# FoX head pairs: where the put-off value and sums transposes stand in the matmul order

## The chip, the cores and the metric

The kernel runs on one core of one Trainium2 chip. The metric is the device time of one execution in microseconds; before the change it is 1346.64 us (median of three runs, 1346.08 to 1347.43). Engines are named as the profile names them: PE multiplies matrices (PEld loads its stationary operand), DVE, ACT and POOL work on vectors, SP issues most DMAs.

## The reference, cut to what matters

One layer of a hybrid decoder trunk on 1024 tokens of width 1024. One projection feeds an HGRN2 head group and a FoX head group (softmax attention with a forget-gate bias, 16 heads of width 64). The change touches only the FoX part: the projection that gives v, and the attention.

```python
def fox_branch(q, k, v, fz, fb):
    q, k, v = heads(q), heads(k), heads(v)
    log_f = jax.nn.log_sigmoid(fz.astype(f32) + fb.astype(f32))
    F = jnp.cumsum(log_f, axis=1).transpose(0, 2, 1)
    for blk in range(S // Q):
        logits = (jnp.einsum('bhtd,bhsd->bhts', qb, kb).astype(f32) * scale
                  + F[:, :, q0:q1, None] - F[:, :, None, :q1])
        probs = jax.nn.softmax(jnp.where(mask, logits, -jnp.inf), axis=-1)
        outs.append(jnp.einsum('bhts,bhsd->bhtd', probs.astype(v.dtype), vb))

u = rmsnorm(h, norm_w[i])
proj = jnp.einsum('bsd,de->bse', u, w_in[i])
hq, hf, hi, hg, fq, fk, fv, fg, fz = jnp.split(proj, SPLIT_POINTS, axis=-1)
y_f = fox_branch(fq, fk, fv, fz, fox_fb[i]) * jax.nn.silu(fg)
y = jnp.concatenate([y_h, y_f], axis=-1)
h = h + jnp.einsum('bse,ed->bsd', y, w_out[i])
```

## The kernel before

The kernel runs in stages: a start (norm, per-layer embedding), the HGRN heads, the FoX heads (about 540 to 1075 us in the profile), and the output projection with the gate and the last norm. Activations are kept transposed, features on partitions and tokens along the free dimension.

**Dense products.** A projection to 128 features is a "dense" job of two products of 512 tokens each (`dense_steps`, `product_steps`, line 355). A product is 24 matmuls of 128x512: eight slices of the contraction (index i), and for each three matmuls (index j) of operands split into a high and a low part (whi, wlo, uhi, ulo). Both halves of the work, the dense jobs of the next pair and the attention of this one, go through PE in one order that the code writes out: `pe` (line 353) keeps PE's instructions in program order. The order on the other engines is set by a scheduler when the program is built; each engine then runs its own list strictly in order.

**The planner.** `Ahead` (line 322) holds the dense jobs as generators. `fill(columns)` (line 343) runs matmuls of the first job until a number of columns is used up; `fill()` without a number runs all that is left. A job's eviction of a product out of PSUM comes when the generator is asked for the step behind the product's last matmul. `weights()` hands out the loaded weights and starts the load of the next (wf by DMA, whi by ACT on line 82, wlo by POOL on line 83). `FOX_FILL` (line 34) gives the columns of a fill: 12288, which is 24 matmuls, while pairs 1 to 4 are worked on, and 9216, which is 18, for pairs 0, 5, 6 and 7.

**Pairs and chunks.** Heads come in eight pairs p of two heads i, each in two chunks c of 512 queries, c = 1 first. The chunks run in a row. `Chunk.mix` (line 878) does for one chunk, twice (part 0 and 1): two groups of logits of the following chunk (line 811, tile lg), half of its own softmax (ACT exponentials on line 847, DVE transposes on line 848), and a fill; then the maxima of the following chunk and its own value products (`values`, line 850, tile po, matmuls on line 859). A copy (avt, line 870, ACT) and an addition (line 871, DVE) bring po to the output tile o. During pair p the jobs of pair p+1 are filled in, in the order k, q, (gate of p), v.

**Put-off steps.** Two kinds of small transposes on PE are not issued where their operands arise but put on the list `ahead.pending`:

- *value transposes* (`fox_v`, line 473): each of the two products of v is copied out to vt (line 480, ACT); the step then transposes vt in four matmuls (line 485), copies the result into the tile v (line 487, ACT), and POOL swaps halves of it into the other rows (`swap`, line 444).
- *sums transposes* (`norms`, line 894): once the exponentials of a head are done, its sums zs go through one matmul (line 900), a copy zk (line 904, ACT), an addition and a reciprocal zt (lines 905 and 908, DVE), a DMA out to zd and a DMA back to rz (lines 910 and 911, SP). rz is what o is multiplied with at the end of a pair (line 918, POOL).

The list is emptied (`flush`, line 334) at three places: behind the first matmul of slice i = 2 of any product (line 360), that is behind its 7th matmul; at the end of a pair, behind `fill()` (line 976); and in the last chunk. The tiles of dense products, of value transposes and of sums transposes come from one PSUM pool of two buffers (pp, tag "proj").

At the end of pairs 0 to 6 the last product of v has its eviction only when `fill()` is called behind the value products. So its value transposes are issued there, by the flush at the pair's end.

Of the kernel before, what the change touches and what calls it, by code (L numbers as in the profile page):

```python
# [64 lines left out]
def trunk(ctx: ExitStack, tc: tile.TileContext, a, out):  # L65
# [85 lines left out]
    with ExitStack() as st:  # L151
# [137 lines left out]
        for c in range(NCH):  # L289
            for k in range(KT):  # L290
# [6 lines left out]
                if c == 0 and k in (2, 4, 6, 7):  # L297
                    i = 8 + (2, 4, 6, 7).index(k)
# [23 lines left out]
    class Ahead:  # L322
# [8 lines left out]
            self.loaded = load and load()  # L331
            return w

        def flush(self):

            while self.pending:
                self.pending.pop(0)()

        def until(self, mark):
            while mark not in self.done:  # L340
# [14 lines left out]
    def product_steps(ps, terms, cost):  # L355
        n = len(terms)
        for i, (whi, wlo, uhi, ulo) in enumerate(terms):
            for j, (x, y) in enumerate(((whi, uhi), (whi, ulo), (wlo, uhi))):
                pe(mm(ps, x, y, start=i == j == 0, stop=i == n - 1 and j == 2))  # L359
                if i == 2 and j == 0:  # L360
                    ahead.flush()
                yield cost

    def dense_steps(mov, evac):
        whi, wlo = ahead.weights()
        for c in range(NCH):
            ps = pp.tile([P, CH], F32, name="ps", tag="proj")
            yield from product_steps(ps, [(whi[:, j], wlo[:, j], *mov[c][j]) for j in range(KT)], CH)
            evac(c, ps)

    def w_in_loads():
        tiles = [T_HQ, T_HG]
        for h in range(HEADS_H - 1):
            tiles += [T_HF + h + 1, T_HQ + h + 1, T_HG + h + 1] + ([-(h + 2)] if h % 2 == 0 and h < HEADS_H - 2 else [])
        tiles += [T_FQ, T_FG, T_FK, T_FV]
        for p in range(PAIRS_F - 1):
            tiles += [T_FK + p + 1, T_FQ + p + 1] + ([T_FG + p] if 0 < p < FIRST_LATE else []) + [T_FV + p + 1]
        tiles += [T_FG + p for p in range(FIRST_LATE, PAIRS_F)]
        for t in tiles:
            yield (lambda t=t: load_w(a["w_in"][t], KT)) if t >= 0 else (lambda t=t: load_pair(T_HI - t))  # L380
        yield lambda: load_w(a["w_out"][0], KT, nc.vector)

    ahead = Ahead(w_in_loads(), first_f)
# [45 lines left out]
    def fox_gate(p):  # L429
        sg = sg_t.setdefault(p, None) or fi.tile([P, S], F32, name="sg")  # L430
        sg_t[p] = sg

        def ev_g(c, ps):
            sl = slice(c * CH, (c + 1) * CH)
            nc.scalar.activation(sg[:, sl], ps, AF.Tanh, scale=0.5)
            nc.vector.scalar_tensor_tensor(out=sg[:, sl], in0=sg[:, sl], scalar=1.0, in1=ps, op0=ALU.add, op1=ALU.mult)

        yield from dense_steps(u, ev_g)
        ahead.done.add(("gate", p))

    def swap(dst, src):

        for r in range(2):
            nc.gpsimd.tensor_scalar(out=dst[r], in0=src[r], scalar1=1.0, scalar2=1.0, op0=ALU.mult, op1=ALU.mult)
# [16 lines left out]
    def fox_k(p):  # L461

        k = k_t[p] = [fp.tile([P, S], F32, name="k", tag="k", bufs=4) for _ in range(2)]

        def ev_k(c, ps):
            sl = slice(c * CH, (c + 1) * CH)
            nc.scalar.copy(k[0][:, sl], ps)
            swap([k[1][half[r], sl] for r in range(2)], [k[0][half[1 - r], sl] for r in range(2)])

        yield from dense_steps(u, ev_k)  # L470
        ahead.done.add(("k", p))

    def fox_v(p):


        v = v_t[p] = fp.tile([P, 2 * FB, P], F32, name="v")

        def ev_v(c, ps):
            vt = fp.tile([P, CH], F32, name="vt", tag="tmp")
            nc.scalar.activation(vt, ps, AF.Copy, scale=0.5)  # L480

            def transposes():
                pt = pp.tile([P, CH], F32, name="ps", tag="proj")
                for b in range(4):
                    pe(nc.tensor.transpose(pt[:, b * P : (b + 1) * P], vt[:, b * P : (b + 1) * P], ident))
                dst = v[:, 8 * c : 8 * c + 8].rearrange("p (b r) d -> p b r d", r=2)
                nc.scalar.copy(dst[:, :, 0], pt.rearrange("p (b d) -> p b d", d=P))
                swap([dst[half[r], :, 1] for r in range(2)], [dst[half[1 - r], :, 0] for r in range(2)])

            ahead.pending.append(transposes)  # L490

        yield from dense_steps(u, ev_v)
        ahead.done.add(("v", p))


    with ExitStack() as st:
# [244 lines left out]
        gates, values = [], [(v, None)]  # L741
# [24 lines left out]
    with fox as st:  # L766
# [4 lines left out]
        class Chunk:  # L771
# [122 lines left out]
            def norms(self, rz):  # L894

                zs = z_t[self.head]

                def transpose():
                    pz = pp.tile([P, CH], F32, name="ps", tag="proj")
                    pe(nc.tensor.transpose(pz[: 2 * FB, :P], zs, ident))  # L900
                    zt = fp.tile([2 * FB, 64], F32, name="zt", bufs=1)
                    zk = fp.tile([2 * FB, 64], F32, name="zk", bufs=1)
                    src = pz[: 2 * FB, :P].rearrange("m (h a q) -> m h a q", h=2, a=2)
                    nc.scalar.copy(zk.rearrange("m (h q) -> m h q", h=2), src[:, :, 0])
                    nc.vector.tensor_tensor(
                        out=zt.rearrange("m (h q) -> m h q", h=2), in0=src[:, :, 1], in1=zk.rearrange("m (h q) -> m h q", h=2), op=ALU.add
                    )
                    nc.vector.reciprocal(out=zt, in_=zt)
                    row = zd[self.head : self.head + 1, :]
                    nc.sync.dma_start(out=row.rearrange("o (b t) -> (o b) t", t=64), in_=zt)  # L910
                    nc.sync.dma_start(out=rz[half[self.i]], in_=row.to_broadcast([64, S]))

                ahead.pending.append(transpose)

        def finish(p, by_gate):
            o = y_t[p]
            if not by_gate:
                nc.gpsimd.tensor_tensor(out=o, in0=o, in1=rz_t.pop(p), op=ALU.mult)
            else:
                nc.gpsimd.tensor_tensor(out=o, in0=o, in1=sg_t[p], op=ALU.mult)  # L920
                (nc.sync if p < PAIRS_F - 1 else nc.gpsimd).dma_start(out=yd[KT + p], in_=o)

        def gate_late(p):
            yield from fox_gate(p)
            if p < PAIRS_F - 1:
                finish(p, True)
# [15 lines left out]
        def y_load(pool, tag, bufs, num=1):  # L942
            t = pool.tile([P, num, S], F32, name=f"yf{len(y_f32)}", tag=tag, bufs=bufs)
            for i in range(num):
                nc.sync.dma_start(out=t[:, i], in_=yd[len(y_f32)])
                y_f32.append(t[:, i])

        for n, ch in enumerate(chunks):
            p, i, c = ch.p, ch.i, ch.c
            following = chunks[n + 1] if n + 1 < len(chunks) else None  # L950
            if i == 0 and c == NCH - 1:
                rz_t[p] = fp.tile([P, S], F32, name="rz", bufs=1)
                if p == PAIRS_F - 1:
                    y_t[p] = o7
                    y_t[FIRST_LATE] = fp.tile([P, S], F32, name="olate", tag="k", bufs=4)
                    nc.sync.dma_start(out=y_t[FIRST_LATE], in_=yd[KT + FIRST_LATE])
                    ahead.jobs += [gate_late(p - 2), gate_late(p - 1), fox_gate(p)]
                    for x in ((fp, "k", 4), (fi, "q", 2), (fp, "v", 2, 2)):
                        y_load(*x)
                else:  # L960
                    if p:
                        y_t[p] = fi.tile([P, S], F32, name="o")
                    ahead.jobs += [fox_k(p + 1), fox_q(p + 1)]
                    if 0 < p < FIRST_LATE:
                        ahead.jobs.append(fox_gate(p))
                    ahead.jobs.append(fox_v(p + 1))
            if c == NCH - 1 and n + 2 < len(chunks):
                chunks[n + 2].biases()
            if following and following.p > p:
                ahead.until(("k", p + 1))  # L970
            if n == len(chunks) - 1:
                y_load(fp, "pt1", 1, 4)
            ch.mix(following)
            if i == 1 and c == 0:
                ahead.fill()
                ahead.flush()
                finish(p, False)
                if p == FIRST_LATE:
                    nc.sync.dma_start(out=yd[KT + p], in_=y_t[p])
                elif p != PAIRS_F - 2:  # L980
                    finish(p, True)
# [173 lines left out]
```

## Time and profile before

| what | value |
|---|---|
| median of the runs | 1346.64 us |
| the profiled execution | 1351.1 us |
| its span, first to last instruction | 1349.2 us |
| mean granted clock of PE | 0.982 |
| PE busy in the FoX stage (540 to 1075 us) | 506.86 of 535 us |
| ACT busy there | 234.47 us |
| DVE busy there | 345.22 us |
| POOL busy there | 176.25 us |

Durations below come from the profiled execution. In the timeline a row has the start in us from the span's start, the length in us, the engine, the line of the kernel, the operation with output and inputs, how many instructions it merges, and in brackets how long the engine sat idle before it and what it waited for. SPq is a DMA issued from SP's queue. fp32 matmuls count twice in the profile (L859 x32 are 16 matmuls of the program).

### The profile page before, as it was taken

How to read it: one execution, taken by the hardware profiler on the slowest of the kernel's cores; microseconds unless marked ns; L12 is line 12 of the kernel's file. 1: busy time of each engine (PE TensorE's matmuls, PEld its weight loads, DVE VectorE, ACT ScalarE, POOL GpSimd, SP SyncE). 2: the span in 40 equal slices, each digit the busy share in tenths (PEclk: the TensorE clock that was granted, in tenths of full speed). 3: DMA queues.
4: the chain of work that ended last, by engine and by line, in shares of the span. 5: the costliest groups of instructions: out<-in, count | busy, mean ns of one | idle time of the engine just before them, and what ended most of it. 6: DMA issues, size and time to landing. Idle time of an engine off the chain costs nothing.

```text
span 1349.2 us, 26805 instructions
## 1 busy us (share of the span) xinstructions
PE 1284.5 (95%) x10996; PEld 1024.2 (76%) x10996; DVE 794.6 (59%) x1988; ACT 475.2 (35%) x1144; POOL 350.4 (26%) x288
## 2 busy tenths in 40 slices
PE   6999999999999999998999999999889999999996
PEld 4887888888888878666767676766667688888895
DVE  6746575656646575575656565667586833333465
ACT  5413132212312133444444444444353512212455
POOL 3613122212212122324242424233322200101232
PEclk9899999999999999998999999999899999999998
DMA  7312111101111112112112111211232453212312
GB/s 283 128 47 64 49 32 64 63 18 61 36 46 51 32 48 70 58 56 71 56 64 64 66 62 56 71 56 56 70 97 87 151 208 110 86 52 70 129 68 74
DMA packets 38970, 102.22 MB, mean 76 GB/s; under 512 B 6720, under 2 KB 8896, under 8 KB 38848
## 3 DMA queue, kind: packets, MB, share of 16 engines
q1 hardware_dynamic: 38704, 99.99, 22.3%
q8 instruction: 86, 1.41, 0.4%
q0 software_dynamic: 144, 0.52, 0.1%
q14 instruction: 36, 0.29, 0.1%
HBM read 83.07 MB, written 17.43 MB: 74 GB/s over the span
## 4 chain that ended last, share of the span: by engine, by line
PE 78%; DVE 10%; ACT 7%; issue 2%; DMA 2%; POOL 1%; SPq 0%; DVEq 0%; ACTq 0%; POOLq 0%
PE ps L359 45%; PE lg L811 5%; PE ps L98 4%; PE ps L100 4%; PE ps L99 4%; PE po L859 4%; ACT x L847 3%; DVE x L825 2%; PE ps L566 1%; PE gps L98 1%; PE gps L99 1%; PE gps L100 1%; DVE x L275 1%; PE po L707 1%; PE po L709 1%
## 5 line engine op out<-in xcount | busy, mean ns | idle before, releaser
L359 PE MATMUL ps<-uhi,whi 128*128 128x512 f32 x896 | 362.8, 405 | 0.0
L359 PE MATMUL ps<-ulo,whi 128*128 128x512 f32 x896 | 355.3, 397 | 0.0
L359 PE MATMUL ps<-uhi,wlo 128*128 128x512 f32 x896 | 354.2, 395 | 0.0
L83 POOL TENSOR_TENSOR wlo<-wf,whi 128x1024 fp32r<-128x1024 f32 x59 | 144.6, 2451 | 481.8 <-ACT whi L82 459.6
L359 PEld LDWEIGHTS ps<-uhi,whi 128*128 128x128 f32 x896 | 169.7, 189 | 60.3 <-issue 25.9
L359 PEld LDWEIGHTS ps<-uhi,wlo 128*128 128x128 f32 x896 | 169.8, 190 | 36.6 <-issue 1.1
L359 PEld LDWEIGHTS ps<-ulo,whi 128*128 128x128 f32 x896 | 170.0, 190 | 33.5 <-issue 0.7
L825 DVE CUSTOM_DVE_ANT_0 x<-lg,fb 128x512 f32<-128x512 f32 (+15 forms) x256 | 101.8, 433 | 111.6 <-PE lg L811 104.9
L82 ACT CAST whi<-wf 128x1024 fp32r<-128x1024 f32 (+1 forms) x77 | 79.6, 1035 | 207.5 <-PE ps L99 89.9
L847 ACT ACTIVATE x<-x,mxo 128x512 f32<-128x512 f32 (+15 forms) x256 | 130.3, 511 | 59.5 <-DVE mxo L835 59.5
L848 DVE STREAM_TRANSPOSE pt<-x 128x512 f32<-128x512 f32 (+15 forms) x256 | 115.4, 459 | 36.3 <-ACT x L847 32.3
L98 PE MATMUL ps<-yhi,whi 128*128 128x512 f32 x256 | 99.8, 390 | 1.8 <-DVE h L1007 1.8
L99 PE MATMUL ps<-ylo,whi 128*128 128x512 f32 x256 | 99.7, 390 | 0.2 <-DVE ylo L83 0.2
L100 PE MATMUL ps<-yhi,wlo 128*128 128x512 f32 x256 | 99.6, 389 | 0.0
L811 PE MATMUL lg<-k,q 64*32 64x480 f32 (+15 forms) x1024 | 77.7, 411 | 2.5 <-DVE mx L825 2.5
L811 PE MATMUL lg<-k,qx 64*32 64x512 f32 (+15 forms) x1024 | 78.2, 413 | 0.0
L859 PEld LDWEIGHTS po<-pt,v 64*64 64x64 f32 x1536 | 53.6, 133 | 22.7 <-issue 9.2
L859 PE MATMUL po<-pt,v 64*64 64x256 f32 (+7 forms) x1536 | 69.4, 320 | 0.0
L98 PEld LDWEIGHTS ps<-yhi,whi 128*128 128x128 f32 x256 | 48.0, 188 | 12.2 <-ACT whi L82 2.2
L99 PEld LDWEIGHTS ps<-ylo,whi 128*128 128x128 f32 x256 | 48.0, 188 | 10.4 <-DVE ylo L83 0.6
L100 PEld LDWEIGHTS ps<-yhi,wlo 128*128 128x128 f32 x256 | 48.1, 188 | 10.0
L359 PE MATMUL ps<-wthi,uhi 128*128 128x256 f32 x192 | 54.0, 281 | 0.0
(205 smaller groups left out, 2160.6 us busy)
## 6 DMA issues: line engine op xcount, KB each, us to landing
wf<-in_w_in_dram SPq DMA_DIRECT2D x64, 512.0 KB, 3.5
fb<-fd SPq DMA_DIRECT2D x64, 128.0 KB, 3.0
yf<-yd SPq DMA_DIRECT2D x16, 512.0 KB, 5.6
wf<-in_w_out_dram SPq DMA_DIRECT2D x16, 512.0 KB, 3.6
x<-in_xT_dram SPq DMA_DIRECT2D x8, 512.0 KB, 9.4
pled<-pleo SPq DMA_DIRECT2D x16, 256.0 KB, 2.9
yd<-sg SPq DMA_DIRECT2D x8, 512.0 KB, 2.6
rz<-zd SPq DMA_DIRECT2D x16, 256.0 KB, 3.4
```

What stands on the lines that cost most here:

```text
L82: pin(nc.scalar.copy(hi, src))
L83: pin(lo_engine.tensor_tensor(out=lo, in0=src, in1=hi, op=ALU.subtract))
L98: pin(mm(ps, whi, uhi, start=i == 0, stop=False))
L99: pin(mm(ps, whi, ulo, start=False, stop=False))
L100: pin(mm(ps, wlo, uhi, start=False, stop=i == n - 1))
L275: nc.vector.scalar_tensor_tensor(out=x, in0=x, scalar=norm_w[:, k : k + 1], in1=rs[c], op0=ALU.mult, op1=ALU.mult)
L359: pe(mm(ps, x, y, start=i == j == 0, stop=i == n - 1 and j == 2))
L811: mm(ps[32 * j : 32 * j + 32, m % 2, : 32 * n], q[:, 32 * (j // 2) :][:, :32], k[not own][rows].rearrange("p (t a k) -> p t a k", a=2, k=3 ...
L825: nc.vector.tensor_tensor_reduce(out=x, in0=ps[:, m % 2, : 32 * n], in1=copies[m % 2][:, : 32 * n], scale=1.0, scalar=BIG, op0=ALU.add, op ...
L847: nc.scalar.activation(x, x, AF.Exp, bias=self.other[:, g : g + 1], scale=-1.0, accum_out=zs[:, m : m + 1])
L848: nc.vector.transpose(self.probs[:, : m + 1, g], x.rearrange("p (t k) -> p t k", k=32))
L859: mm(po[half[t % 2], r, 32 * first : 256], v_t[self.p][half[r], t ^ r, half[self.i]], self.probs[half[r], t, first:].rearrange("p g q -> p ...
```

## The change

The list now holds a kind beside each step ("values" or "sums"), and `flush` can be told which kinds and how many. Inside a product there are three places for a step instead of one, behind the 7th, the 13th and the 19th matmul, and each place issues at most one step, the oldest. At a pair's end only steps of the kind "sums" are issued; a value step that is left stays on the list until the next dense product. The last chunk still empties the whole list.

```diff
@@ class Ahead
-        def flush(self):
-
-            while self.pending:
-                self.pending.pop(0)()
+        def put_off(self, kind, step):
+            self.pending.append((kind, step))
+
+        def flush(self, *kinds, most=None):
+
+            steps = [x for x in self.pending if not kinds or x[0] in kinds][:most]
+            self.pending = [x for x in self.pending if x not in steps]
+            for _, step in steps:
+                step()
@@ product_steps
-                if i == 2 and j == 0:
-                    ahead.flush()
+                if i in (2, 4, 6) and j == 0:
+                    ahead.flush(most=1)
@@ fox_v
-            ahead.pending.append(transposes)
+            ahead.put_off("values", transposes)
@@ Chunk.norms
-                ahead.pending.append(transpose)
+                ahead.put_off("sums", transpose)
@@ the loop over the chunks
             if i == 1 and c == 0:
                 ahead.fill()
-                ahead.flush()
+                ahead.flush("sums")
                 finish(p, False)
```

Lines behind `flush` move down by five (L485 is L490 after the change, L359 is L364). What moves on PE stands the same way at the ends of pairs 0 to 6. At the end of pair 0, PE's order before, around the value products (po), the value transposes (from vt) and the first logits of pair 1's second chunk (lg):

```order
L359 MATMUL ps_5962<-uhi_305,wlo_5647 128x512
L859 MATMUL po_6043<-pt0_5876,v_5289 64x256 x4
...
L859 MATMUL po_6043<-pt0_5876,v_5289 64x32 x2
L485 MATMUL ps_6065<-cst_307,vt_6063 128x128 x4
L811 MATMUL lg_6090<-k_5461,qx_5643 32x256
...
L811 MATMUL lg_6102<-k_5460,q_5642 32x160
L359 MATMUL ps_6130<-uhi_275,whi_5853 128x512
L359 MATMUL ps_6130<-ulo_276,whi_5853 128x512
```

and after the change:

```order
L364 MATMUL ps_5962<-uhi_305,wlo_5647 128x512
L864 MATMUL po_6043<-pt0_5876,v_5289 64x256 x4
...
L864 MATMUL po_6043<-pt0_5876,v_5289 64x32 x2
L816 MATMUL lg_6082<-k_5461,qx_5643 32x256
...
L816 MATMUL lg_6094<-k_5460,q_5642 32x160
L364 MATMUL ps_6122<-uhi_275,whi_5853 128x512
...
L364 MATMUL ps_6122<-uhi_279,whi_5853 128x512
L490 MATMUL ps_6130<-cst_307,vt_6063 128x128 x4
L364 MATMUL ps_6122<-ulo_280,whi_5853 128x512
```

The four value transposes moved from ahead of the logits to behind the 7th matmul of the next dense product.

In the product before that one, the last of pair 0, both kinds of steps are on the list. PE's order there before (value transposes from vt, then the sums transpose from zs), and after:

```order
L359 MATMUL ps_5962<-uhi_295,whi_5646 128x512
L485 MATMUL ps_6002<-cst_307,vt_5960 128x128 x4
L900 MATMUL ps_6010<-cst_307,zs_5419 16x128
L359 MATMUL ps_5962<-ulo_296,whi_5646 128x512
L359 MATMUL ps_5962<-uhi_295,wlo_5647 128x512
```

```order
L364 MATMUL ps_5962<-uhi_295,whi_5646 128x512
L490 MATMUL ps_6002<-cst_307,vt_5960 128x128 x4
L364 MATMUL ps_5962<-ulo_296,whi_5646 128x512
...
L364 MATMUL ps_5962<-uhi_299,whi_5646 128x512
L905 MATMUL ps_6016<-cst_307,zs_5419 16x128
L364 MATMUL ps_5962<-ulo_300,whi_5646 128x512
```

The second step moved six matmuls down. In pairs 1 to 4 the sums come first and the value transposes are the ones that move down; pairs 5 and 6 are like pair 0.

ACT's order at the end of pair 0 before (exponentials of the next chunk on tile x1, the weight cast whi, the copies avt and vt), and after:

```order
L904 COPY zk_6013<-ps_6010 16x64
L847 ACTIVATE x1_5914,zs_5746<-x1_5914,mxo_6036 128x512
...
L847 ACTIVATE x1_5914,zs_5746<-x1_5914,mxo_6036 128x352
L82 CAST whi_6126<-wf_6124 128x1024
L847 ACTIVATE x1_5914,zs_5746<-x1_5914,mxo_6036 128x320
L847 ACTIVATE x1_5914,zs_5746<-x1_5914,mxo_6036 128x288
L870 COPY avt_6060<-po_6043 64x512
L480 ACTIVATE vt_6063<-ps_5962 128x512
```

```order
L852 ACTIVATE x1_5914,zs_5746<-x1_5914,mxo_6036 128x512
L909 COPY zk_6019<-ps_6016 16x64
...
L82 CAST whi_6118<-wf_6116 128x1024
L852 ACTIVATE x1_5914,zs_5746<-x1_5914,mxo_6036 128x384
...
L852 ACTIVATE x1_5914,zs_5746<-x1_5914,mxo_6036 128x320
L875 COPY avt_6060<-po_6043 64x512
L485 ACTIVATE vt_6063<-ps_5962 128x512
L852 ACTIVATE x1_5914,zs_5746<-x1_5914,mxo_6036 128x288
```

vt and avt moved ahead of the last exponential, zk behind the first, the cast two exponentials up. This is so at pairs 0, 5 and 6; at pairs 1 to 4 avt and vt stay behind the last exponential.

On SP, at pairs 0, 5 and 6, the DMA of rz (line 911) moved behind the next weight load (line 88): before, the three DMAs stood in the order zd, rz, wf; now in the order zd, wf, rz. That weight load waits for the buffer that POOL's wlo (line 83) reads. On POOL, one of the two swaps of v at pairs 0, 5 and 6, and both at pairs 1 to 4, now stand behind the multiplication of o with rz, and at pairs 1 to 4 behind the one with the gate too.

## The prediction

> **What bounds the kernel now.** I read the page first, for the share of each engine, then the waits of PE in the FoX stage (540 to 1075 us), then the timeline at single pair ends, and last the granted clock around them.
>
> ```profile
> span 1349.2 us, 26805 instructions
> PE 1284.5 (95%) x10996; PEld 1024.2 (76%) x10996; DVE 794.6 (59%) x1988; ACT 475.2 (35%) x1144; POOL 350.4 (26%) x288
> ```
>
> PE is the bound: it is busy for 95% of the span, so a microsecond counts when it is taken from PE's waits or from the length of its matmuls. The waits of PE in the FoX stage (what waited, on what; microseconds in all, times, longest) are these four groups:
>
> ```profile
> PE ps L485 <- ACT vt L480: 18.8, 7, 3.9
> PE ps L485 <- DVE zt L905: 4.8, 4, 1.2
> PE lg L811 <- DVE mx L825: 2.5, 5, 1.0
> PE ps L900 <- ACT v L487: 2.0, 3, 0.7
> ```
>
> Three of the four stand before a put-off step: the value transposes (L485) and the sums transpose (L900). Together they are 18.8 + 4.8 + 2.0 = 25.6 us in 14 places, and seven of these are the ends of pairs 0 to 6. The timeline shows why, at the end of pair 0 (start, length, what; idle time before it in brackets):
>
> ```profile
> 608.39 0.28 PE L900 MATMUL ps<-cst,zs 128*16 128x128 f32 x1 [0.68 <-ACT v L487]
> 608.71 0.20 ACT L904 COPY zk<-ps 16x64 f32<-16x64 f32 x1 [0.37 <-PE ps L900]
> 612.49 1.31 PE L859 MATMUL po<-pt,v 64*64 64x256 f32 x32
> 614.27 1.03 ACT L82 CAST whi<-wf 128x1024 fp32r<-128x1024 f32 x1
> 615.76 0.52 ACT L847 ACTIVATE x<-x,mxo 128x288 f32<-128x288 f32 x1
> 616.40 0.58 ACT L870 COPY avt<-po 64x512 f32<-64x512 f32 x1
> 617.00 0.60 ACT L480 ACTIVATE vt<-ps 128x512 f32<-128x512 f32 x1
> 617.65 1.11 PE L485 MATMUL ps<-cst,vt 128*128 128x128 f32 x4 [3.85 <-ACT vt L480]
> ```
>
> PE has nothing left after the value products (po) at 613.80, because the next instruction in its order is the value transposes. They need vt, which ACT does last: the exponentials of the next chunk's softmax, a weight cast and avt stand ahead of it, and it ends at 617.60. The logits of the next chunk, ready to run, are queued behind.
>
> The stall has a second price. The windows below each run from the value transposes of a pair end to the logits behind the first stretch of dense matmuls (columns: length, busy time of PE, PEld, DVE, ACT, POOL, granted clock, DMA share, GB/s). The work in one is transposes, two groups of logits and 24 dense matmuls (18 in the last three).
>
> ```profile
> 617.65:627.13 9.48, 9.48 (x68) 6.78 (x75) 1.90 (x11) 0.58 (x1) 6.13 (x6) 0.74 0.32 113
> 687.22:695.96 8.74, 8.74 (x61) 6.17 (x61) 1.90 (x11) 0.59 (x1) 6.69 (x6) 0.80 0.28 105
> 756.05:763.23 7.18, 7.17 (x61) 5.39 (x61) 1.90 (x11) 0.59 (x1) 6.73 (x6) 1.00 0.23 73
> 823.33:832.10 8.77, 8.77 (x61) 6.29 (x61) 1.90 (x11) 0.59 (x1) 6.70 (x6) 0.81 0.31 105
> 892.19:898.02 5.83, 5.83 (x55) 4.26 (x55) 1.90 (x11) 0.59 (x1) 5.60 (x6) 1.00 0.29 93
> 950.69:959.42 8.73, 8.73 (x54) 6.06 (x54) 1.90 (x11) 0.58 (x1) 3.75 (x5) 0.63 0.33 120
> 1012.10:1020.86 8.76, 8.76 (x54) 6.08 (x54) 1.90 (x11) 0.58 (x1) 3.74 (x5) 0.63 0.51 181
> ...
> 540.00:615.00 75.00, 72.62 (x734) 50.44 (x732) 51.56 (x174) 33.52 (x97) 24.00 (x26) 1.00 0.17 54
> 623.00:687.00 64.00, 61.19 (x609) 44.65 (x607) 38.39 (x134) 27.86 (x83) 17.48 (x18) 1.00 0.18 59
> 692.00:823.00 131.00, 125.34 (x1258) 91.58 (x1256) 78.69 (x278) 56.36 (x167) 41.91 (x40) 1.00 0.19 62
> 828.00:949.00 121.00, 114.77 (x1211) 82.75 (x1209) 79.09 (x274) 53.45 (x161) 38.97 (x39) 1.00 0.20 63
> 958.00:1011.00 53.00, 49.19 (x555) 34.68 (x553) 39.55 (x131) 25.40 (x79) 13.90 (x16) 1.00 0.28 81
> 1019.00:1075.00 56.00, 54.75 (x528) 40.97 (x527) 43.72 (x118) 29.35 (x79) 12.85 (x6) 1.00 0.31 104
> ```
>
> After five of the seven ends the granted clock is below 1; everywhere else in the stage it is 1.00. The two ends that kept it give the undisturbed lengths, 7.18 us with 24 matmuls and 5.83 us with 18. The excess is 2.30, 1.56 and 1.59 us for pairs 0, 1 and 3, and 2.90 and 2.93 us for pairs 5 and 6: 11.3 us in all.
>
> **The change part by part.** The instructions of each kind stay the same; some move.
>
> (a) *Value transposes at a pair end.* They leave the place ahead of the next logits and stand behind the 7th matmul of the next dense product. The wait of 18.8 us goes, and what can be late next is vt at the new place. When PE gets there is read at pair 2, whose clock is full:
>
> ```profile
> 748.48 0.66 PE L485 MATMUL ps<-cst,vt 128*128 128x128 f32 x4 [1.18 <-DVE zt L905]
> ...
> 756.05 0.66 PE L485 MATMUL ps<-cst,vt 128*128 128x128 f32 x4 [1.81 <-ACT vt L480]
> 756.64 0.40 PE L811 MATMUL lg<-k,qx 64*32 64x256 f32 x1
> ...
> 757.55 0.51 PE L359 MATMUL ps<-uhi,whi 128*128 128x512 f32 x1
> ...
> 759.28 0.39 PE L359 MATMUL ps<-ulo,whi 128*128 128x512 f32 x1
> ```
>
> The logits take 757.55 - 756.64 = 0.91 us and seven dense matmuls 759.28 - 757.55 = 1.73 us, so PE reaches the transposes 2.64 us after the values' end. Pairs 0, 5 and 6: the values end 0.68 us sooner by (b), at 613.12 for pair 0, and PE arrives at 615.76. ACT now does vt ahead of the last exponential (616.40 - 615.76 = 0.64 us earlier) and with one small copy, zk, more ahead of it (0.20 us): it ends at 617.16, the transposes start 0.05 us later, and PE waits 1.45 us. Pairs 1 to 4: at pair 2 the stall began at 756.05 - 1.81 = 754.24 and begins 1.18 us sooner by (b); PE arrives at 755.70, and vt, whose place hardly moves, releases it at 756.05: 0.35 us, and about the same (0.36) in the four. New waits: 3 x 1.45 + 4 x 0.36 = 5.8 us. Their bounds are 0 and the old 18.8; I take 5.8, since PE's arrival and the end of vt both come from rows. Queued behind a waiting transpose are the other 17 (or 11) matmuls of the product, nothing else.
>
> (b) *Two steps in one product.* Before, both put-off steps stood behind the 7th matmul, and the second waited for the buffer that the first one's copy releases: 4.8 us (pairs 1 to 4) and 2.0 us (0, 5, 6). Now the second stands six matmuls later, 6 x 0.23 = 1.4 us; the waits were at most 1.25 and 0.68 us, so both go: 6.8 us. Below that, six matmuls cover them; if a copy is late the whole 6.8 us could come back, and no more.
>
> (c) *The clock.* With the long stall gone I expect no drop, a gain of 11.3 us. The bounds are 0 and 11.3. In this trace waits of 0.28 to 1.25 us at a time (the mx, zt and v groups) have no drop behind them, two of four waits of 1.8 us have one, three of three of 3.85 us have a longer one. The new waits, 1.45 us and shorter, lie nearer to the group without.
>
> (d) *Other queues.* On SP, at the ends of pairs 0, 5 and 6, the load of the inverse sums (rz) now stands behind a weight load (wf) that waits for POOL; on POOL one or both swaps of v stand behind the multiplications of o that need rz. Whoever waits is PE, for v, at the value products of the next pair's first chunk. At pair 5:
>
> ```profile
> 945.42 0.45 SPq L911 DMA_DIRECT2D rz<-zd  x1
> 948.48 2.35 POOL L83 TENSOR_TENSOR wlo<-wf,whi 128x1024 fp32r<-128x1024 f32 x1 [5.64 <-ACT whi L82]
> 950.86 0.35 SPq L88 DMA_DIRECT2D wf<-in_w_in_dram  x1
> 950.84 2.38 POOL L918 TENSOR_TENSOR o<-o,rz 128x1024 f32<-128x1024 f32 x1
> 953.30 1.29 POOL L444 TENSOR_SCALAR v<-v 64x512 f32<-64x512 f32 x2
> ...
> rz<-zd SPq DMA_DIRECT2D x16, 256.0 KB, 3.4
> ...
> 964.21 2.16 PE L859 MATMUL po<-pt,v 64*64 64x256 f32 x34
> ```
>
> The weight cast moves two exponentials forward, so wlo ends near 949.9 instead of 950.83; wf is issued, and rz near 950.3, landing 3.4 us later at 953.7, or near 955 if it shares the engines with wf. Then o (2.4 us) and the second swap (0.65) end at 956.8 to 958.2. PE needed 964.21 - 950.69 = 13.52 us from the transposes to po; less the clock's 2.90 and the 2.64 us that now lie ahead of them it is 7.98, so it arrives at 950.25 + 7.98 = 958.2. I cost it at nothing, with bounds 0 and 1 us at each of three ends; the cover is thin, and each microsecond beyond costs one. Pairs 1 to 4 keep their order of DMAs, and the swaps wait only for one more multiplication (2.4 us).
>
> Sum: 25.6 - 5.8 + 11.3 = 31.1 us. The profiled execution took 1351.1 us, so it would take 1320.0; the median of the runs, 1346.64, is 4.5 us lower, and the same difference gives **1315.5 us**.
>
> **The rivals.**
>
> *The clock still falls at some ends.* Two drops followed waits of only 1.8 us while two equal waits left the clock alone, so their place in time seems to matter, and 1.45 us with 0.59 us of transposes behind may do it too, at pairs 0, 5 and 6; or the drops of pairs 1 and 3 had another cause and stay. The price is 1.56 to 1.59 us for each short drop: two to five of them give 1315.5 + 3.2 to 8 = 1318.7 to 1323.5, and the full 11.3 us 1326.8. Against it: every drop in the stage follows a stall. The Trainium skill, TensorE: Matmul & The Clock Gate, "Why this matters for your kernels", asks for "No PE-idle gaps >~3µs between matmul bursts"; by that rule only the 3.85 us stalls could have dropped the clock, and the sum would be 1318.7 us. The trace disagrees at two of the four 1.8 us waits (clock 0.80 and 0.81). The same page, "Part 4: PE-mode transpose", says that transposes do not count as busy for the gate, which would lengthen each gap by its transposes; no run here shows that apart.
>
> *The wait only moves.* If vt is put off on ACT as PE moves on, the transposes stand in the middle of the product as long as before, and the change does not do what it says. For it: they still need the same vt. Against it: PE has 2.64 us of work to put ahead. Price: all of (a) but not (b): 1346.64 - 6.8 = 1339.8, or 1328.5 with the clock's gain.
>
> *Late v.* The swaps come 1 to 3 us too late at pairs 0, 5 and 6: 1318.5 to 1324.5.
>
> *Slower than before.* The same chain, rz behind wf, o behind rz, v behind o, outweighs the gain. It decides from 31.1 / 3 = 10.4 us of lateness at each of the three ends, that is if rz lands about 14 us after its issue where the row has 3.4 us: 1347 us and more. Only the order of the queues speaks for it.
>
> **How the numbers follow.** Forecast (1311 to 1318): 0.59. Clock falls at some ends: 0.21. Late v: 0.08. The wait only moves: 0.06. Slower: 0.03. A new wait smaller than costed or a gain elsewhere, below 1311: 0.03. The range from 1309.5 to 1328 takes in the zero wait of (a) (1309.7) and the full loss of the clock's gain (1326.8) and leaves out about 0.1. About 0.2% (2.7 us) is what a measurement of this kernel can tell from no change. Faster by more: 0.95; within: 0.02; slower: 0.03.
>
> **What would show it.** (a): the wait of L485 for vt near 6 us instead of 18.8, none ahead of the logits at pair ends. (b): the groups waiting for zt and for v gone. (c): granted clock 1.00 through the whole FoX stage and some 7.2 or 5.8 us in windows like those above. (d): no wait of po for POOL. The prediction is wrong if po waits at the first chunk of pairs 1, 6 and 7, if the logits meet a new wait for mx, or if a half clock shows behind short waits.

## The result, and the profile after

| | before | after |
|---|---|---|
| median of four runs each | 1347.04 us (1346.08 to 1348.14) | 1318.72 us (1317.97 to 1319.91) |
| ratio of the runs, 95% interval | | 0.9776 (0.9761 to 0.9791) |
| profiled execution, its span | 1351.1, 1349.2 us | 1317.97, 1316.2 us |
| mean granted clock of PE | 0.982 | 0.994 |

The change makes the kernel 28.3 us faster, with an interval of 28 to 32 us; 31.1 us was forecast. The median of before is now that of four runs; the prediction started from the first three, 1346.64 us. The page's engine row, after:

```profile
PE 1270.2 (97%) x10996; PEld 1014.5 (77%) x10996; DVE 799.8 (61%) x1988; ACT 475.0 (36%) x1144; POOL 351.2 (27%) x288
```

As many matmuls as before take 14.3 us less busy time (1284.5 - 1270.2), which points to the clock; where these 14.3 us lie is shown further down. The waits of PE in the FoX stage, after (what waited, on what; us in all, times, longest):

```profile
PE ps L490 <- ACT vt L485: 6.4, 7, 1.5
PE lg L816 <- DVE mx L830: 2.6, 5, 1.0
```

The groups for zt (4.8 us) and for v (2.0 us) are gone, and the one for vt is 6.4 us instead of 18.8. The timeline at the end of pair 0, PE and ACT:

```profile
614.16 0.58 ACT L875 COPY avt<-po 64x512 f32<-64x512 f32 x1
614.76 0.60 ACT L485 ACTIVATE vt<-ps 128x512 f32<-128x512 f32 x1
615.25 0.53 ACT L852 ACTIVATE x<-x,mxo 128x288 f32<-128x288 f32 x1
...
615.41 0.66 PE L490 MATMUL ps<-cst,vt 128*128 128x128 f32 x4 [1.53 <-ACT vt L485]
```

PE still arrives before vt is ready, but waits only 1.53 us, since the logits and seven dense matmuls of the next product now stand ahead of the transposes. The granted clock in windows of the changed kernel that cover the FoX stage (columns as before; the clock is the third number from the end):

```profile
540.00:612.00 72.00, 71.51 (x758) 49.45 (x756) 49.45 (x172) 32.15 (x93) 22.50 (x24) 1.00 0.16 49
612.00:622.00 10.00, 8.47 (x71) 6.50 (x68) 6.17 (x23) 5.00 (x13) 4.86 (x4) 1.00 0.25 80
622.00:677.00 55.00, 55.00 (x561) 39.95 (x567) 37.70 (x126) 24.49 (x76) 18.67 (x19) 1.00 0.22 69
677.00:690.00 13.00, 12.53 (x114) 9.62 (x99) 7.83 (x33) 5.79 (x16) 9.68 (x8) 1.00 0.30 107
690.00:926.00 236.00, 234.29 (x2473) 169.28 (x2472) 155.64 (x541) 106.33 (x315) 81.96 (x79) 1.00 0.20 64
926.00:938.00 12.00, 10.47 (x88) 7.77 (x91) 9.44 (x32) 4.79 (x13) 6.69 (x6) 1.00 0.26 86
938.00:1055.00 117.00, 111.65 (x1106) 81.79 (x1099) 91.26 (x253) 57.68 (x161) 31.91 (x27) 1.00 0.39 131
```

No drop is left, at the ends of pairs 0, 1 and 5 (second, fourth and sixth window) or elsewhere. And the queues at pair 5, on SP, POOL and PE:

```profile
928.73 0.35 SPq L88 DMA_DIRECT2D wf<-in_w_in_dram  x1
929.18 0.45 SPq L916 DMA_DIRECT2D rz<-zd  x1
...
934.20 2.42 POOL L923 TENSOR_TENSOR o<-o,rz 128x1024 f32<-128x1024 f32 x1 [2.94 <-DMA rz<-zd]
936.70 0.61 POOL L449 TENSOR_SCALAR v<-v 64x512 f32<-64x512 f32 x1
...
937.11 3.03 PE L864 MATMUL po<-pt,v 64*64 64x256 f32 x64
```

rz does stand behind the weight load and POOL does wait for it (2.94 us), as forecast. The second swap ends at 937.31, 0.2 us after PE has begun the value products (937.11), and PE waits for nothing there.

### The profile page after: what moved, and what is told of

It is laid out like the page before. It is cut to its first block, busy times and chain, and to the rows that moved or that the text cites. A ratio compares the mean times of both kernels' runs of the same rounds, so it can differ in the third digit from the quotient of the medians.

```text
span 1316.2 us, 26795 instructions
## 1 busy us (share of the span) xinstructions
PE 1270.2 (97%) x10996; PEld 1014.5 (77%) x10996; DVE 799.8 (61%) x1988; ACT 475.0 (36%) x1144; POOL 351.2 (27%) x288
## 4 chain that ended last, share of the span: by engine, by line
PE 80%; DVE 9%; ACT 6%; issue 2%; DMA 1%; POOL 1%; SPq 0%; DVEq 0%; ACTq 0%; POOLq 0%
PE ps L364 46%; PE lg L816 5%; PE ps L100 4%; PE po L864 4%; PE ps L98 4%; PE ps L99 4%; ACT x L852 2%; PE ps L571 1%; PE gps L100 1%; PE gps L99 1%; PE gps L98 1%; DVE x L275 1%; PE po L712 1%; PE po L714 1%; DVE x L830 1%
## 5 line engine op out<-in xcount | busy, mean ns | idle before, releaser
L364 PE MATMUL ps<-uhi,whi 128*128 128x512 f32 x896 | 360.1, 402 | 0.0
L364 PE MATMUL ps<-ulo,whi 128*128 128x512 f32 x896 | 354.4, 396 | 0.0
L364 PE MATMUL ps<-uhi,wlo 128*128 128x512 f32 x896 | 352.5, 393 | 0.0
L364 PEld LDWEIGHTS ps<-uhi,whi 128*128 128x128 f32 x896 | 168.2, 188 | 58.5 <-issue 21.6
L364 PEld LDWEIGHTS ps<-uhi,wlo 128*128 128x128 f32 x896 | 168.4, 188 | 35.6 <-issue 1.1
L364 PEld LDWEIGHTS ps<-ulo,whi 128*128 128x128 f32 x896 | 168.4, 188 | 33.6 <-issue 0.7
L98 PE MATMUL ps<-yhi,whi 128*128 128x512 f32 x256 | 99.8, 390 | 1.7 <-DVE h L1012 1.7
L816 PE MATMUL lg<-k,q 64*32 64x480 f32 (+15 forms) x1024 | 74.4, 396 | 2.6 <-DVE mx L830 2.6
L816 PE MATMUL lg<-k,qx 64*32 64x512 f32 (+15 forms) x1024 | 74.4, 396 | 0.0
L98 PEld LDWEIGHTS ps<-yhi,whi 128*128 128x128 f32 x256 | 48.0, 188 | 12.2 <-ACT whi L82 2.1
L364 PE MATMUL ps<-wthi,uhi 128*128 128x256 f32 x192 | 54.0, 281 | 0.0
```

The lines of the kernel that those rows point to most:

```text
L98: pin(mm(ps, whi, uhi, start=i == 0, stop=False))
L816: mm(ps[32 * j : 32 * j + 32, m % 2, : 32 * n], q[:, 32 * (j // 2) :][:, :32], k[not own][rows].rearrange("p (t a k) -> p t a k", a=2, k=3 ...
```

## The experiments

The theory: PE is the bound; the gain is the waits before put-off steps (25.6 - 6.4 = 19.2 us) plus the clock that the stalls at pair ends cost. Its rivals: the drops of the clock have another cause; the wait only moves; v comes late. The kernel before was timed beside each of them, on the same chip.

**One part of the change alone.** First the flush at a pair's end, with the old place inside a product (these two edits start from the changed kernel):

```diff
-                if i in (2, 4, 6) and j == 0:
-                    ahead.flush(most=1)
+                if i == 2 and j == 0:
+                    ahead.flush()
```

> Only the flush at a pair's end is changed (sums alone); inside a product both put-off steps stay behind the 7th matmul. Theory (the gain is the pair-end wait plus the clock that it costs): the 6.8 us of waits for zt and v stay, the 18.8 us for vt become about 3 x 1.2 us (PE brings 2.64 us of work ahead of transposes whose vt is as late as before), the granted clock is 1.00 through the FoX stage; 15 us of waits and about 9 us of clock, so about 1323 us. Rival (the clock does not depend on the stall): 15 us, about 1332 us. Rival (the wait only moves): about 1347 us.

Measured: 1324.46 us beside 1350.72 us of the kernel before, a ratio of 0.9807 (0.9793 to 0.9820), 26.3 us less where about 24 were expected. The granted clock is 1.00 through the FoX stage. The waits of PE in this kernel:

```profile
PE ps L490 <- DVE zt L910: 4.8, 4, 1.2
PE ps L490 <- ACT vt L485: 3.5, 3, 1.2
PE lg L816 <- DVE mx L830: 2.5, 5, 1.0
PE ps L905 <- ACT v L492: 2.0, 3, 0.7
```

The waits that the second part would take are untouched, vt costs 3.5 us (3.6 expected), and 18.8 - 3.5 = 15.3 us of waits leave 26.3 - 15.3 = 11 us for the clock (9 expected). Both rivals fall: they had a gain of 15 us and none.

Then the places inside a product alone, with everything issued at a pair's end:

```diff
-                ahead.flush("sums")
+                ahead.flush()
```

> Only the places inside a product are changed (one step behind the 7th, the next behind the 13th matmul); a pair's end still issues everything. Theory (at a pair's end PE waits for ACT, which does not care how early PE comes): the waits for zt and v, 6.8 us, go, but the wait for vt grows by as much less what ACT brings forward (0.64 us less zk at pairs 0, 5 and 6): about 24 us of waiting for vt, the clock drops stay, a gain of 0 to 1.5 us, 1345.5 to 1347 us. Rival (the two parts add up): 6.8 us less, 1340 us.

Measured: 1352.46 us beside 1350.72, a ratio of 1.0020 (1.0009 to 1.0031): not a gain but a small loss. The waits of PE and, in the windows behind it, the clock after the ends of pairs 0 to 6:

```profile
PE ps L490 <- ACT vt L485: 25.4, 7, 4.3
PE lg L816 <- DVE mx L830: 2.6, 5, 1.0
```

```profile
616.50:623.50 7.00, 6.69 (x48) 4.70 (x49) 2.69 (x12) 1.36 (x4) 2.90 (x3) 0.58 0.38 116
688.00:694.00 6.00, 6.00 (x43) 4.50 (x28) 1.85 (x10) 0.00 (x0) 4.79 (x4) 0.78 0.26 91
756.00:761.00 5.00, 5.00 (x46) 3.33 (x45) 1.84 (x10) 0.59 (x1) 4.77 (x4) 0.71 0.32 105
824.00:831.00 7.00, 6.76 (x46) 4.71 (x47) 2.14 (x11) 0.77 (x2) 6.35 (x6) 0.53 0.24 75
895.00:900.00 5.00, 5.00 (x44) 3.64 (x44) 1.85 (x10) 0.59 (x1) 4.77 (x4) 0.66 0.35 108
954.00:960.00 6.00, 5.95 (x44) 4.07 (x45) 2.43 (x12) 1.10 (x3) 2.54 (x3) 0.50 0.41 131
1015.00:1021.00 6.00, 5.97 (x49) 4.24 (x50) 2.40 (x12) 1.08 (x3) 2.05 (x3) 0.73 0.86 268
```

The 6.8 us of waits for zt and v went, and the wait for vt grew by 6.6 us, from 18.8 to 25.4: PE came earlier to the same late vt. The two parts do not add up. The loss of 1.7 us, which I had not expected, goes with the clock: in the profiled execution it fell behind all seven ends, where the kernel before kept it at pairs 2 and 4.

**The clock by itself.** Matmuls whose result nobody reads are put into the stall of the kernel before. In the trace the order of ACT and DVE stays as it was; on POOL the multiplication with the gate moves ahead of a swap at some pair ends. So it is PE's idleness that changes. Added ahead of the flush at a pair's end:

```diff
+                if following:
+                    idle = lg.tile([P, 2, CH], F32, name="lg", tag="lg")
+                    for _ in range(6 if 0 < p < 5 else 14):
+                        pe(mm(idle[:, 0], u[0][0][0][:, :P], u[0][1][0], start=True, stop=True))
```

> The kernel before, with matmuls of 128x512 whose result nobody reads put into the stall at each pair's end (14 at pairs 0, 5 and 6, 6 at pairs 1 to 4), ahead of the value transposes. They need no more than the stall (14 x 0.23 = 3.2 us in 3.85 us), so waits and order stay as before and only PE's idleness is changed. Theory (the idle stall drops the granted clock): clock 1.00 through the FoX stage and 7 to 11 us less, about 1338 us. Rival (the drops have another cause): same time within 2 us.

Measured: 1339.87 us beside 1350.72, a ratio of 0.9920 (0.9908 to 0.9932): 10.9 us less for 66 more matmuls (3 x 14 + 4 x 6). The end of pair 0 on PE (filler, then value transposes), and the stage's clock:

```profile
612.70 1.31 PE L859 MATMUL po<-pt,v 64*64 64x256 f32 x32
613.93 3.47 PE L979 MATMUL lg<-uhi 128*128 128x512 f32 x14
617.87 0.66 PE L485 MATMUL ps<-cst,vt 128*128 128x128 f32 x4 [0.47 <-ACT vt L480]
```

```profile
540.00:1076.00 536.00, 521.50 (x5217) 377.46 (x5216) 352.71 (x1173) 236.60 (x683) 177.93 (x167) 1.00 0.23 76
```

From the end of the value products to the value transposes it is 3.86 us (614.01 to 617.87), against 3.85 us before, so the stall is as long, only filled. The idle stall drops the clock, and that costs 10.9 us (9 to 12 by the interval), against 11.3 us read from the windows of one execution.

The same with transposes as filler:

```diff
-                    for _ in range(6 if 0 < p < 5 else 14):
-                        pe(mm(idle[:, 0], u[0][0][0][:, :P], u[0][1][0], start=True, stop=True))
+                    for _ in range(9 if 0 < p < 5 else 23):
+                        pe(nc.tensor.transpose(idle[:, 0, :P], ident, ident))
```

> As the kernel with dense filler, but the filler is transposes of 128x128 (23 and 9 of them, 0.14 to 0.15 us each) instead of dense matmuls. If any work on PE counts against the drop of the clock, as in the dense filler: about 1338 us and clock 1.00. If transposes do not count as busy, as the Trainium skill says (TensorE: Matmul & The Clock Gate, Part 4: PE-mode transpose): the drops stay, about 1347 us. The theory of the clock leaves this open.

Measured: 1340.01 us beside 1350.72, a ratio of 0.9920 (0.9908 to 0.9932), like the dense filler. The end of pair 0 and the clock behind it:

```profile
613.90 2.73 PE L979 MATMUL lg<-cst 128*128 128x128 f32 x23
617.84 0.66 PE L485 MATMUL ps<-cst,vt 128*128 128x128 f32 x4 [1.21 <-ACT vt L480]
```

```profile
617.84:624.00 6.16, 6.16 (x56) 4.82 (x57) 1.90 (x11) 0.59 (x1) 5.93 (x6) 1.00 0.31 106
```

Transposes keep the clock up, with 1.21 us of idleness left here; the granted clock is 1.00 behind the other pair ends too.

**What is left.** PE still waits 6.4 us for vt. The runs that go after it were timed on two other chips, each beside the kernel before. First the changed kernel itself:

> The changed kernel itself, beside the same runs of the kernel before as the two that follow. Theory (waits 25.6 - 6.4 = 19.2 us, and the clock that the dense filler measured, 10.9 us): 30.1 us less than the kernel before, about 1320.6 us where that one takes 1350.7. Rival (the clock's part is the 9.1 us that the first comparison left): 28.3 us less.

Measured: 1319.86 us beside 1351.22, a ratio of 0.9775 (0.9759 to 0.9790): 31.4 us less, nearer to 30.1 than to 28.3. The ratio is nearly that of the first comparison (0.9776), whose interval (28 to 32 us) holds the theory's figure and the rival's, so theory and rival cannot be told apart.

To take the 6.4 us too, the places were moved six matmuls down:

```diff
-                if i in (2, 4, 6) and j == 0:
+                if i in (4, 6) and j == 0:
```

> The changed kernel with its places for put-off steps behind the 13th and the 19th matmul instead of the 7th, 13th and 19th. Six matmuls more (1.36 us) lie ahead of the value transposes of a pair's end, and ACT brings vt another exponential forward at pairs 0, 5 and 6, so the 6.4 us of waits for vt go. Theory (v is only just ready at pairs 5 and 6, because rz stands behind a weight load): PE then waits there for POOL's swaps, which now both stand behind the multiplication with rz and end about 2.3 us after PE arrives; 6.4 - 4.6 = about 2 us less than the changed kernel, and a new wait of po for POOL near 4.6 us. Rival (PE alone counts): 6.4 us less and no wait for POOL.

Measured: 1317.00 us beside 1351.22, a ratio of 0.9754 (0.9738 to 0.9770), 2.9 us less than the changed kernel. The amount fits, but for another reason. The waits of PE, and POOL and PE at pair 5:

```profile
PE ps L490 <- DVE zt L910: 2.6, 4, 0.6
PE ps L905 <- ACT v L492: 2.1, 3, 0.7
PE ps L98 <- DVE h L1012: 1.7, 1, 1.7
PE lg L816 <- DVE mx L830: 1.1, 2, 0.8
```

```profile
936.26 1.32 POOL L449 TENSOR_SCALAR v<-v 64x512 f32<-64x512 f32 x2
...
936.00 3.03 PE L864 MATMUL po<-pt,v 64*64 64x256 f32 x64
```

The wait for vt is gone (L98 is the stage behind). The 4.6 us of waiting for POOL that I expected are not there: po starts at 936.00 while the swaps run until 937.58. The value products of this chunk go through 16 key slots in order, and the half of v that is swapped last belongs to slots 8 to 15, so it is needed about half of 3.03 us later. Instead the second put-off step now waits for zt and v again (2.6 + 2.1 us), since ACT copies zk and v one exponential later in this kernel's order: at pair 0, v stood ahead of the first exponential and now stands behind it. By the groups: 6.4 - 2.6 - 2.1 + (2.6 - 1.1, fewer waits for mx) = 3.2 us.

With the sums first on the list:

```diff
+            steps = sorted((x for x in self.pending if not kinds or x[0] in kinds), key=lambda x: x[0] != "sums")[:most]
```

> The later places, and where both kinds are on the list the sums first. Then rz is asked for ahead of the weight load at pairs 0, 5 and 6 too, and the multiplication of o with it starts some 4 us sooner. Theory: no wait for vt, none for POOL, 6.4 us less than the changed kernel and faster than both. Rival (v is late for another reason than rz): a wait of po for POOL stays, about 2 us less than the changed kernel.

Measured: 1314.58 us (1313.36 to 1314.77) beside 1351.22, a ratio of 0.9734 (0.9718 to 0.9750) and 5.3 us less than the changed kernel timed with it (1319.66 to 1319.97). The waits for v are gone as well; the four for zt stay:

```profile
PE ps L490 <- DVE zt L910: 2.6, 4, 0.6
PE ps L98 <- DVE h L1012: 1.7, 1, 1.7
PE lg L816 <- DVE mx L830: 1.1, 2, 0.8
```

By the groups, 6.4 - 2.6 + (2.6 - 1.1) = 5.3 us, as measured. No run had a wait of po for POOL that an earlier rz could have taken away; what changed is which of the two steps meets which copy. Two more runs, on the other of these two chips, go further. The second place three matmuls further down:

```diff
-                if i in (4, 6) and j == 0:
+                if i in (4, 7) and j == 0:
```

> As the later places with the sums first, but the second place is behind the 22nd matmul instead of the 19th. The profile of that kernel still has four waits of about 0.65 us for zt before the second step (pairs 1 to 4); three matmuls more are 0.68 us. Theory (a put-off step costs PE only what it comes early): those 2.6 us go and nothing else is late, a ratio to the kernel before of 0.9715, some 2.5 us less than with the 19th. Rival (zt moves on as the step does): the same time as with the 19th, a ratio of 0.9734.

Measured: 1310.90 us (1310.15 to 1311.93) beside 1350.02, a ratio of 0.9712 (0.9699 to 0.9725), 39.1 us faster than the kernel before and the lowest ratio of all. It was not timed beside the run with the 19th, and the two intervals overlap; that the 2.6 us went is read from the waits, of which only these are left:

```profile
PE ps L98 <- DVE h L1012: 1.7, 1, 1.7
PE lg L816 <- DVE mx L830: 1.1, 2, 0.8
```

And the sums first with the places of the change:

```diff
-                if i in (4, 6) and j == 0:
+                if i in (2, 4, 6) and j == 0:
```

> The changed kernel with its own three places (7th, 13th, 19th matmul), only that the sums go first where both kinds are on the list. Theory (v was never late, rz did not cost PE anything): the wait for vt at pairs 0, 5 and 6 shrinks by what ACT brings forward, one exponential of about 0.65 us each, and all else stays: 1 to 2 us less than the changed kernel, a ratio of 0.976 to 0.977. Rival (an early rz was what made the later places pay): most of their gain already here, a ratio near 0.974.

Measured: 1318.21 us beside 1350.02, a ratio of 0.9763 (0.9749 to 0.9776). Its waits before put-off steps:

```profile
PE ps L490 <- ACT vt L485: 3.9, 7, 0.7
...
PE ps L490 <- DVE zt L910: 0.5, 3, 0.2
```

2.5 us less of waiting for vt and 0.5 us more for zt. The ratio lies in the range expected, and its interval still holds the changed kernel's 0.9775. By the waits, the order alone takes 2.0 us, the later places alone took 3.2 us, and both together 5.3 us, so most comes from the places; the times alone do not separate the three.

## Why the prediction was right, point by point

The mechanism and each term were right. The time was not quite: 1318.72 us lies 0.7 us above the forecast of 1311 to 1318. By the time alone it would be the first rival with two short drops (1318.7); the granted clock of 1.00 in its profile rules that out.

*(a), value transposes at a pair's end.* Right. 5.8 us of new waits were forecast, 6.4 measured: 1.53 us at pair 0 (1.45 forecast) and 0.43 to 0.47 us at pairs 1 to 4 (0.36). The run with this part alone shows it by itself.

*(b), two steps in one product.* The 6.8 us of waits went, as forecast. But the sum treated them as a gain of their own, and the run with this part alone shows that they are none: 6.6 of them moved into the wait for vt. In the sum this was right because (a) already counted PE's earlier arrival, 0.68 or 1.18 us, against itself.

*(c), the clock.* The mechanism is shown by the two fillers. Its size, 11.3 us, was that of one execution; the filler measured 10.9 us. The clock differs from run to run: on the chip of the fillers the slowest run of the kernel before, 1352.67 us, has a mean clock of 0.982, and the fastest, 1347.40 us, one of 0.987. The Trainium skill (TensorE: Matmul & The Clock Gate, "Why this matters for your kernels") puts the limit at gaps over about 3 us; the traces agree for the long gaps and differ below, since two of four gaps of 1.8 us had a drop behind them.

*(d), other queues.* Right that it costs nothing. PE was forecast to arrive 7.98 us after the transposes and came after 7.91 (937.11 - 929.20). rz landed later than its median of 3.4 us: POOL waited for it until 5.0 us after its issue. By the prediction's own rule, that PE waits until the swaps end, 0.2 us would have been lost at pair 5. None was, because po's first matmuls do not need the half of v that is swapped last; the cost of nothing was right partly by luck.

*The step that was off* is the last one, from the profiled execution to the runs. Between the profiled executions the sum came out. From the first value transposes of the FoX stage to the first matmul of the stage behind it (columns as before):

```profile
552.86:1079.45 526.59, 496.55 (x5042) 357.79 (x5041) 345.83 (x1163) 234.25 (x680) 170.60 (x161) 0.97 0.22 72
...
551.05:1046.49 495.44, 484.40 (x5042) 350.05 (x5041) 351.15 (x1163) 233.98 (x680) 171.39 (x161) 1.00 0.24 76
```

The stage is 31.15 us shorter (31.1 forecast): 12.15 us of it is busy time of PE (11.3 forecast for the clock), 19.0 us idle time (25.6 - 5.8 = 19.8 forecast). The other 1.8 us between the two executions, and with them 2.1 of the 14.3 us of busy time, lie ahead of this stage. There the profiled execution of before has half a clock from 59.4 to 62.8 us, which the one of after lacks; seven of the nine other profiles have such a spell too, with and without the change, so it belongs to the execution and not to the change.

The sum, taken from the profiled 1351.1 us, gave 1320.0 us. Then 4.5 us were taken off, because the profiled execution of before had been that much longer than its three runs. The measured median is 1318.72 us, 3.2 us above the 1315.5 so reached and 1.3 us below the sum, and the profiled execution of after, 1317.97 us, is no longer than its runs: the difference did not carry over. Beside the later runs the kernel before took 1350.02 to 1351.22 us, so its first three runs lay at the lower end of what it takes. That the spread of before is made of drops of the clock fits the clocks on record (0.982 to 0.987) but was not shown by a run of its own.

*The rivals.* "The clock still falls" did not happen: no wait of the changed kernel is above 1.53 us, and none has a drop behind it. "The wait only moves" fell; its price of 1339.8 us was wrong as well, since it counted (b) as a gain while the wait for vt stays, and that run gained nothing. "Late v" had the right chain but not the price, as the later places show. "Slower" needed rz to land 14 us after its issue; it took 5.

## What to carry to other kernels

Taking a wait away is worth only what the next wait leaves of it: here 6.8 us taken away ahead of a copy that did not come sooner gave nothing, because PE waited as much longer for that copy. Where PE stalls for 1.8 us or more, look for the granted clock in windows behind the stall, since here it added 11 us to 19 us of waiting. A small step that waits for another engine went best behind enough dense matmuls to cover the copy, one step at a time; how many more are needed was read from the wait that remained (0.65 us of wait, three matmuls).

## What the runs showed of the hardware

The clock's drop depends on the length of the idle time. Over the profiled executions of before, of the places alone and of the change, the 14 waits of 0.43 to 1.53 us ahead of put-off steps had no drop right behind them, those of about 1.8 us had one in 2 of 4 cases, those of 3.14 to 3.17 us in 4 of 4, and those of 3.85 and 4.25 us in 6 of 6.

Equal waits differ in part because of where they fall. In the clock records of all eleven profiles the clock changes only on a fixed grid of 3.41 us, and each spell at half clock within the program lasts one or two of its steps: before, 615.75 to 622.58 us at pair 0 and 687.43 to 690.85 at pair 1, and the 64.85 us between them are 19 steps. So count PE's idle time step by step, in the FoX stage, in steps that begin at full clock: with 1.96 us or more, half a clock followed in 10 of 10 steps (before and the places alone); with 1.78 to 1.81 us in 2 of 3 (before); with 1.77 us or less in none, in any of the eleven. The 1.81 us at pair 2 that kept the clock lie across the edge of a step (1.46 us ahead of it); why the 1.81 us at pair 4, all in one step, kept it stays open. It follows for these traces that no wait of 1.53 us could have dropped the clock by itself, wherever it fell.

Transposes count as work for the clock: 2.73 us of transposes in the stall kept the clock at 1.00 as 3.47 us of dense matmuls did. The Trainium skill (TensorE: Matmul & The Clock Gate, "Part 4: PE-mode transpose") has it that transposes do not count as busy in the same way; in these runs they did.
